# A hybrid RWKV-7 and convolution layer on one core: joined matmul bursts, the convolution moved forward, and dense products issued six at a time

## The chip, the cores and the metric

The kernel runs on one core of a Trainium2 chip. The metric is the time of one execution on the device in microseconds (us). Three timed runs of the kernel before took 1325.54, 1330.57 and 1337.1 us, and their median is 1330.57 us. TensorE, the matmul array, is called PE in the profile; VectorE is DVE, ScalarE is ACT, GpSimd is POOL, and SyncE (SP) issues the transfers.

## The reference

One layer for 640 tokens (512 latent and 128 context ones) of width 1024, cut to its products and the two branches:

```python
def _wkv(s0, r, w, k, v, a, b, reverse):
...
    def step(S, inp):
        rt, wt, kt, vt, at, bt = inp
        sa = jnp.einsum('bhvk,bhk->bhv', S, at)
        S = S * wt[:, :, None, :] + sa[..., None] * bt[:, :, None, :] + vt[..., None] * kt[:, :, None, :]
        return S, jnp.einsum('bhvk,bhk->bhv', S, rt)
...
    s_fin, ys = lax.scan(step, s0.astype(jnp.float32), xs, reverse=reverse)
...
def _conv_branch(glu_in, rows, lp):
    a, gt = jnp.split(glu_in, 2, axis=-1)
    u = a * jax.nn.sigmoid(gt)
...
    u = lax.conv_general_dilated(u, lp['conv_w'][:, None, :], (1,), [(CONV_K // 2, CONV_K // 2)],
                                 dimension_numbers=('NWC', 'WIO', 'NWC'), feature_group_count=C) + lp['conv_b']
...
    un = ((uf - mu) * lax.rsqrt(var + LN_EPS) * lp['conv_ln_g'] + lp['conv_ln_b']).astype(u.dtype)
    return jax.nn.silu(un) @ lp['w_out_conv']
...
    xn = _rmsnorm(x, lp['norm1_g']) * (1 + sc1) + sh1
    proj = xn @ lp['w_in']
    rkv, glu_in, gates = jnp.split(proj, [3 * RWKV_WIDTH, 3 * RWKV_WIDTH + 2 * CONV_WIDTH], axis=-1)
    gate_r, gate_c = jnp.split(gates, 2, axis=-1)
    y_r, s_f, s_b = _rwkv_branch(xn, rkv, s0_f, s0_b, lp)
    y_c = _conv_branch(glu_in, rows, lp)
    merged = jax.nn.sigmoid(gate_r) * y_r + jax.nn.sigmoid(gate_c) * y_c
    x = x + g1 * (merged @ lp['w_o'])
    xn2 = _rmsnorm(x, lp['norm2_g']) * (1 + sc2) + sh2
    h = jnp.square(jax.nn.relu(xn2 @ lp['mlp_w1']))
    x = x + g2 * (h @ lp['mlp_w2'])
```

## The kernel before

**Dense products.** Every product with a large weight is made in blocks of 128 output columns. Inputs and weights are split into a high and a low part, and each block is three products (high by high, low by high, high by low) over 8 slices of 128 inputs and two halves of 320 tokens, so a block is 48 matmuls of 128x128 by 128x320 (fewer inputs for the two branch outputs). In the profile they are the rows `ps_mm<-xh_t,wh_t` and the like. The rows `ps_mm<-ARGH_t,wh_t` are the products with the outputs of the two branches, called the sides: side "c" is the convolution's, side "r" the RWKV branch's.

**Lanes.** The scan is not run token by token: the 8 heads are taken as four pairs (p = 0 to 3), the tokens in chunks, and each pair goes through `prep` (operands), `gram` (products of operands), `inverse` (inverts 20 triangular matrices, in steps that go between DVE and PE), `builder` (five groups of chunks: matrices from `pb`, `pk`, `pl`, `pf`, `pu`), `chain` inside `scan` (the state is carried from chunk to chunk: `sp` makes a state, `po` an output) and `finish` (`post`: normalisation, bonus, gate). Their matmuls are small fp32 ones (32x32 to 128x128) in bursts of 4 to 40. The convolution (`conv_all`, five tiles of 128 tokens in `conv_tile`) and the modulation columns (`ada_late`) are lanes too. A lane is a generator that yields where it must wait for another engine.

**What sets the order.** All of this, from about 60 us until the sides' products, is recorded in one program order by a planner at build time: the loop at the end of the mixed stage picks a lane that can go on by its urgency, and otherwise takes one dense matmul from `filler` (through `more`), which works off the list `todo`. The order so found is fixed: on the chip each engine takes its instructions in that order and waits where an operand is not there. `todo` holds 36 blocks that need no lane beyond the projections' own (12 of r, k and v, 8 of the convolution's input `glu`, 16 gates), then the side blocks, which wait for the branches: `c` for its first two blocks, `r` for all the rest. Behind the mixed stage stands the MLP, dense blocks alone.

**Names.** `HEADS` and `QUADS` are halves and quarters of the 128 partitions; `GC` = 2 is the number of chunks in a group and direction; `rk[2, p]` is v of a pair; `hold()` and `let_go()` reserve the array's four result banks for one lane; `places` are buffers that weights may be split into. `GLU_AT` is the place in `todo` at which the four `glu` jobs stand.

```python
        while lanes:
            lane = pick(not hungry())
            if not lane and more():
                continue
            lane = lane or pick(True)
```

Of the kernel before, what the change touches and what calls it, by code (L numbers as in the profile page):

```python
# [10 lines left out]
F32 = mybir.dt.float32  # L11
# [47 lines left out]
RAWS, SPLITS, SWITCH, EXTRA = ["vr"], ["N1"], 1, 0  # L59
# [12 lines left out]
CST_ID, CST_MA, CST_MZ, CST_SEL, CST_HSEL, CST_LATE = 0, 128, 256, 512, 514, 516  # L72
NCST = 517
# [5 lines left out]
def hybrid_step(ctx: ExitStack, tc: tile.TileContext, I, O):  # L79
# [78 lines left out]
    mask_a = cst[:, CST_MA:CST_MA + 128]  # L158
# [458 lines left out]
    def ada_late(col):  # L617
# [10 lines left out]
        e = st([P, P], "ade")  # L628
        A.activation(e, ps, AF.Copy)
        yield  # L630
        ps = bank("t")[:, 0:2]
        mm(ps, e, sel)
        A.activation(mod[:, col, :], ps, AF.Identity, bias=pc("ada_b", col))
# [35 lines left out]
    def operands(p):  # L669
# [20 lines left out]
        for d in range(2):  # L690
# [46 lines left out]
            V.tensor_tensor(out=AB[:, ys, 3 * C:4 * C], in0=tv(at), in1=cs, op=ALU.mult)  # L737
# [16 lines left out]

    vr = wt([P, T], "vr")
# [14 lines left out]
    def gram(p):  # L770

        AB = grp[p]["AB"]
        N = grp[p]["N"] = wt([P, NY, C], f"N{p % 2}")
        yield from hold()
        for i, y0 in enumerate((0, 10)):
            ps = bank(BANKS[i])[:, 0:320].rearrange("p (y c) -> p y c", c=32)
            for y in range(y0, y0 + 10):
                for q, rows in enumerate(QUADS):
                    lo, h = HEADS[q // 2][0], 32 * (q % 2)
                    mm(ps[rows, y - y0, :], AB[lo, y, 2 * C + h:2 * C + h + 32], AB[lo, y, h:h + 32], tile_position=(lo.start, rows.start))  # L780
            A.activation(Gf[:, y0:y0 + 10, :], ps, AF.Copy)
            yield "A"
        for i, y0 in enumerate((0, 10)):
            ps = bank(UP_BANKS[i])[:, 0:320].rearrange("p (y c) -> p y c", c=32)
            for y in range(y0, y0 + 10):
                for s in range(2):
                    lo, rows = HEADS[s][0], QUADS[2 * s]
                    mm(ps[rows, y - y0, :], AB[lo, y, 2 * C:2 * C + 32], AB[lo, y, 32:64], tile_position=(lo.start, rows.start))
            for s in range(2):
                A.activation(N[QUADS[2 * s], y0:y0 + 10, 32:64], ps[QUADS[2 * s]], AF.Copy)  # L790
                yield "A"
        let_go()
        yield SEM
# [5 lines left out]
    def inverse(p):  # L799
# [68 lines left out]
        def products(lhsT, rhs, c0):  # L868
            ps = bank("t")[:, 0:160].rearrange("p (y j) -> p y j", j=16)
            for c in range(10):  # L870
                for q in QUADS:
                    mm(ps[q, c], lhsT[q, c0 + c, :], rhs[q, c0 + c, 0:16], tile_position=(q.start, q.start))
            return ps

        for c0 in (0, 10):
            A.activation(M[:, c0:c0 + 10], products(Gf, Nd, c0), AF.Copy, scale=late)
            yield
        for c0 in (0, 10):
            o = Nd[:, c0:c0 + 10, 0:16]
            V.tensor_tensor(out=o, in0=products(NT, M, c0), in1=o, op=ALU.add)  # L880
            yield

        def quads(f):

            ps = bank("t")[:, 0:320].rearrange("p (y c) -> p y c", c=32)
            for y in range(10):
                for s in range(2):
                    q0, q1 = QUADS[2 * s:2 * s + 2]
                    f(ps[q1, y, :], y, q0, q1)
            return ps  # L890

        for q in range(4):
            A.activation(N[QUADS[q], :, 32 * (q % 2):32 * (q % 2) + 32], Nd[QUADS[q], 0:NY, :], AF.Copy)
            yield "A"
        Tm = tmp.rearrange("p i x -> p (i x)")[:, 640:960].rearrange("p (y t) -> p y t", t=32)
        for y0 in (0, 10):
            ps = quads(lambda o, y, q0, q1: mm(o, Nd[q1, y0 + y, :], ident[q1, q1], tile_position=(q1.start, q1.start)))
            for s in range(2):
                q1 = QUADS[2 * s + 1]
                A.activation(NT[q1, y0:y0 + 10, :], ps[q1], AF.Copy)  # L900
            yield
            ps = quads(lambda o, y, q0, q1: mm(o, N[q0, y0 + y, 32:64], Nd[q0, y0 + y, :], tile_position=(q0.start, q1.start)))
            for s in range(2):
                q1 = QUADS[2 * s + 1]
                A.activation(Tm[q1], ps[q1], AF.Copy)
            yield
            ps = quads(lambda o, y, q0, q1: mm(o, NT[q1, y0 + y, :], Tm[q1, y, :], tile_position=(q1.start, q1.start)))
            for s in range(2):
                q0, q1 = QUADS[2 * s:2 * s + 2]
                A.activation(N[q1, y0:y0 + 10, 0:32], ps[q1], AF.Copy)  # L910
                G.memset(N[q0, y0:y0 + 10, 32:64], 0.0)
            yield
# [104 lines left out]
    def chain(p):  # L1017
# [6 lines left out]
        for g in range(5):  # L1024
# [3 lines left out]
            for i in range(GC):  # L1028
                if (g, i) == (3, GC - 1):
                    break  # L1030
# [620 lines left out]
```

## Time and profile before

| | us |
|---|---|
| median of three timed runs | 1330.57 |
| profiled execution | 1323.99 |
| its span | 1322.2 |
| PE busy in the span | 1236.1 (93%) |
| DVE busy | 654.0 (49%) |
| ACT busy | 505.3 (38%) |

The profiled execution is 6.6 us below the median. PE is busy for 93% of the span, and 86% of the chain that ended last lies on it, so the time is read as a sum along PE: what it does, at which clock, and where it stands still. The span has three parts: a prelude to about 60 us, the mixed stage to about 800 us, and the dense stage to 1320 us.

### The profile page before, as it was taken

To read this page: it belongs to the slowest core of one execution; us is meant where nothing else is said; L and a number is where in the kernel's file an instruction comes from. 1 tells how busy PE (TensorE), PEld (TensorE's weight loads), DVE (VectorE), ACT (ScalarE), POOL (GpSimd) and SP (SyncE) were. 2 spreads that over 40 slices of the span, in tenths; PEclk is the share of its full clock that TensorE was granted. 3 is DMA by queue.
4 is the path that set the end of the run, shared out by engine and by line. 5 is a ranking of instruction groups with operands and counts; after the bars stand their busy time and mean duration, and the time that the engine had idled before them with its cause. 6 is when DMAs were issued, how large, how long until landed. Compare 5 with 4: busy or idle time off the path is not lost.

```text
span 1322.2 us, 30685 instructions
## 1 busy us (share of the span) xinstructions
PE 1236.1 (93%) x13110; PEld 1094.7 (83%) x13110; DVE 654.0 (49%) x1342; ACT 505.3 (38%) x1149; POOL 31.4 (2%) x38
## 2 busy tenths in 40 slices
PE   8998899999999999999974899999999999999996
PEld 5776788777777878877741899999999999999996
DVE  5424575376465656245433566654443443443344
ACT  4445346436443643544212223344421331242130
POOL 0000000000000000100100000000000000000000
PEclk8989899999999999999976899989999999999998
DMA  9465433224222311231300683202222222222222
GB/s 371 144 207 171 149 117 122 78 67 150 80 78 81 124 43 58 87 92 54 100 26 8 209 286 122 74 32 78 73 75 81 72 72 81 80 71 74 81 73 80
DMA packets 77785, 136.14 MB, mean 103 GB/s; under 512 B 10768, under 2 KB 27824, under 8 KB 77648
## 3 DMA queue, kind: packets, MB, share of 16 engines
q1 hardware_dynamic: 77648, 134.17, 30.9%
q8 instruction: 103, 1.69, 0.5%
q14 instruction: 34, 0.28, 0.1%
HBM read 112.90 MB, written 21.23 MB: 101 GB/s over the span
## 4 chain that ended last, share of the span: by engine, by line
PE 86%; DVE 4%; ACT 3%; issue 3%; DMA 2%; SPq 0%; POOL 0%; POOLq 0%; DVEq 0%; ACTq 0%
PE ps_mm L195 45%; PE ps_b L195 21%; PE ps_t L195 12%; PE ps_a L195 6%; PE ps_ad L195 2%; DMA z<-tmp 1%; ACT Nb_w L108 1%; DMA par_t<-in_par 1%; DVE E_w L108 1%; DVE Gt_w L108 1%; ACT tmp L108 0%; DVE ARGH_t L108 0%; DMA g<-tmp 0%; DVE Gf_w L108 0%; ACT N_w L108 0%
## 5 line engine op out<-in xcount | busy, mean ns | idle before, releaser
L195 PE MATMUL ps_mm<-xh_t,wh_t 128*128 128x320 f32 x664 | 219.9, 331 | 1.2 <-ACT tmp L108 1.2
L195 PE MATMUL ps_mm<-xl_t,wh_t 128*128 128x320 f32 x664 | 219.8, 331 | 0.0
L195 PE MATMUL ps_mm<-xh_t,wl_t 128*128 128x320 f32 x664 | 217.1, 327 | 0.0
L108 ACT ACTIVATE wh_t<-wr_t 128x512 fp32r<-128x512 f32 x150 | 94.3, 629 | 141.0 <-PE ps_b L195 107.7
L108 DVE TENSOR_TENSOR wl_t<-wr_t,wh_t 128x512 fp32r<-128x512 f32 x150 | 102.8, 686 | 90.6 <-ACT wh_t L108 90.4
L195 PEld LDWEIGHTS ps_mm<-xh_t,wh_t 128*128 128x128 f32 x664 | 128.1, 193 | 19.8 <-issue 14.4
L195 PEld LDWEIGHTS ps_mm<-xl_t,wh_t 128*128 128x128 f32 x664 | 128.2, 193 | 14.6 <-issue 10.8
L195 PEld LDWEIGHTS ps_mm<-xh_t,wl_t 128*128 128x128 f32 x664 | 127.9, 193 | 12.4 <-issue 9.0
L195 PE MATMUL ps_mm<-ARGH_t,wh_t 128*128 128x320 f32 x284 | 77.8, 319 | 11.7 <-ACT wh_t L108 10.9
L108 ACT ACTIVATE tmp<-ps_mm 128x320 f32<-128x320 f32 x80 | 34.9, 436 | 96.7 <-PE ps_mm L195 90.8
L195 PE MATMUL ps_mm<-ARGH_t,wl_t 128*128 128x320 f32 x212 | 67.4, 318 | 0.0
L195 PEld LDWEIGHTS ps_mm<-ARGH_t,wh_t 128*128 128x128 f32 x284 | 53.1, 199 | 12.4 <-ACT wh_t L108 11.1
L108 ACT ACTIVATE mwh<-wr_t 128x512 fp32r<-128x512 f32 x49 | 31.1, 634 | 74.5 <-PE ps_b L195 69.9
L108 DVE TENSOR_TENSOR mwl<-wr_t,mwh 128x512 fp32r<-128x512 f32 x49 | 33.8, 690 | 38.6 <-ACT mwh L108 38.6
L108 DVE TENSOR_TENSOR tmp<-tmp 128x320 f32<-128x320 f32 x64 | 31.2, 489 | 42.7 <-ACT tmp L108 42.7
L108 DVE SCALAR_TENSOR_TENSOR ARGH_t<-ps_mm,mod_t,ARGH_t 128x320 f32<-128x320 f32 (+2 forms) x45 | 22.6, 511 | 59.4 <-PE ps_mm L195 59.4
L195 PE MATMUL ps_mm<-xl,wh_t 128*128 128x320 f32 x140 | 43.9, 314 | 0.0
L195 PE MATMUL ps_b<-ARGH_t,wl_t 128*128 128x320 f32 x140 | 43.2, 308 | 0.0
L195 PE MATMUL ps_b<-xl,wh_t 128*128 128x320 f32 x140 | 43.1, 308 | 0.0
L195 PE MATMUL ps_b<-ARGH_t,wh_t 128*128 128x320 f32 x140 | 42.6, 304 | 0.0
L195 PEld LDWEIGHTS ps_mm<-ARGH_t,wl_t 128*128 128x128 f32 x212 | 41.5, 196 | 0.4 <-DVE wl_t L108 0.4
L108 DVE SCALAR_TENSOR_TENSOR ARGH_t<-ps_b,mod_t,ARGH_t 128x128 f32<-128x128 f32 (+1 forms) x75 | 26.3, 390 | 20.0 <-PE ps_b L195 20.0
(372 smaller groups left out, 3027.6 us busy)
## 6 DMA issues: line engine op xcount, KB each, us to landing
wr_t<-in_w SPq DMA_DIRECT2D x225, 256.0 KB, 2.8
adl_w<-in_adal SPq DMA_DIRECT2D x64, 256.0 KB, 3.3
adar_s<-in_adaw SPq DMA_DIRECT2D x16, 512.0 KB, 8.4
ARGH_t<-in_x SPq DMA_DIRECT2D x8, 640.0 KB, 5.8
z<-tmp SPq DMA_DIRECT2D x32, 160.0 KB, 3.0
gate<-tmp SPq DMA_DIRECT2D x32, 160.0 KB, 1.8
tA_t<-z SPq DMA_DIRECT2D x8, 320.0 KB, 3.4
ath_t<-z SPq DMA_DIRECT2D x8, 320.0 KB, 3.4
```

What stands on the lines that cost most here:

```text
L108: return f(*args, **kw)
L195: PE.matmul(out=out, lhsT=lhsT, rhs=rhs, start=start, stop=stop, **kw)
```

## The change

- `todo`: the four `glu` jobs stand at place 3 and not 12, right behind the first pair's projections.
- The main loop: where it takes a dense matmul, it takes up to six in a row (`STAY`).
- The convolution runs as soon as `glu` is done: `conv_tile` works in the tiles `pa`, `pg`, `N1` and `cy` and writes its result to memory (`conv0` to `conv3`); a new lane `conv_branch` loads it again later, splits it and opens side "c". `solve(p)`, which runs `gram` and `inverse`, waits for a first mark of the convolution (its constants), and for pair 1 also until all five tiles are done; `finish` waits for the tiles too.
- Bursts are joined: `gram` issues its 120 matmuls in one burst of four rows where it had four bursts; `inverse` joins each pair of products (80 matmuls instead of 2 of 40), makes its transposes with one DVE operation per pair instead of 8 bursts of PE, and has two bursts of 40 where it had four of 20 beside those; `build` issues v, `pb`, `pk` and `pl` in one burst (v reversed is not made any more: the operand is stored reversed, and two masks depend on the direction); `chain` issues a chunk's state and output products together; `ada_late` adds four columns at a time.

```diff
+STAY = 6
...
-GLU_AT = 12
+GLU_AT = 3
...
-        for i, y0 in enumerate((0, 10)):
-            ps = bank(BANKS[i])[:, 0:320].rearrange("p (y c) -> p y c", c=32)
-            for y in range(y0, y0 + 10):
-                for q, rows in enumerate(QUADS):
-                    lo, h = HEADS[q // 2][0], 32 * (q % 2)
-                    mm(ps[rows, y - y0, :], AB[lo, y, 2 * C + h:2 * C + h + 32], AB[lo, y, h:h + 32], tile_position=(lo.start, rows.start))
-            A.activation(Gf[:, y0:y0 + 10, :], ps, AF.Copy)
-            yield "A"
+        for y in range(NY):
+            for q, rows in enumerate(QUADS):
+                lo, h = HEADS[q // 2][0], 32 * (q % 2)
+                mm(near[y // 10][rows, y % 10, :], AB[lo, y, 2 * C + h:2 * C + h + 32], AB[lo, y, h:h + 32], tile_position=(lo.start, rows.start))
+        for y in range(NY):
+            for s in range(2):
+                lo, rows = HEADS[s][0], QUADS[2 * s]
+                mm(far[y // 10][rows, y % 10, :], AB[lo, y, 2 * C:2 * C + 32], AB[lo, y, 32:64], tile_position=(lo.start, rows.start))
...
+        V.transpose(out=NT, in_=Nd)
...
+        for q, ys, ps in quads(BANKS, lambda o, y, q0, q1: mm(o, N[q0, y, 32:64], Nd[q0, y, :], tile_position=(q0.start, q1.start))):
+            A.activation(Tm[q, ys], ps, AF.Copy)
...
-            ps = quads(lambda o, y, q0, q1: mm(o, Nd[q1, y0 + y, :], ident[q1, q1], tile_position=(q1.start, q1.start)))
...
     def solve(p):
-        while p not in operated or (p and p - 1 not in inverted) or (p > 1 and p - 2 not in built):
+        while p not in operated or len(convolved) < 1 + (p == 1) or (p and p - 1 not in inverted) \
+                or (p > 1 and p - 2 not in built):
             yield 0.3
...
     def finish(p):
-        while p and p - 1 not in scanned:
+        while len(convolved) < 2 or (p and p - 1 not in scanned):
...
-        while 3 not in inverted:
-            yield 0.5
...
-        while 2 not in built or 3 not in operated:
-            yield 0.3
...
+        convolved.append(0)
+        for i in range(4):
+            while i not in gated_linear:
+                yield 1.0
...
+            yield from conv_tile(i, u, ut, pr)
+        convolved.append(1)
+        spawn(conv_branch(), URGENT["branch"])
...
+    def conv_branch():
+
+        while 2 not in built or 3 not in operated:
+            yield 0.3
+        un = st([P, 2, 4, T], "ARGH", 2, F32R)
+        for j in range(4):
+            t = st([P, T], f"ath{j % 2}")
+            DMA.dma_start(out=t, in_=dram(f"conv{j}"))
+            yield 2.5 if j == 0 else 0.5
+            split(un[:, 0, j, :], un[:, 1, j, :], t)
...
             if not lane and more():
+                for _ in range(STAY - 1):
+                    if not more():
+                        break
                 continue
```

In all PE has 9251 matmuls and not 9411 (the 160 transposes are gone), and its order changes between dense and lane matmuls 320 times and not 617 times; the dense matmuls are the same 5712. SP issues 24 transfers more (20 writes of the convolution's tiles and 4 loads).

On PE, at the first pair's `gram` (`ps_a<-ARGH_t 32x32` and `ps_b<-ARGH_t 32x32`; the other rows are dense products), before:

```order
L195 MATMUL ps_mm<-xh_t,wh_t 128x320
L195 MATMUL ps_a_1468<-ARGH_t 32x32 x40
L195 MATMUL ps_mm<-xl_t,wh_t 128x320
L195 MATMUL ps_b_1512<-ARGH_t 32x32 x40
L195 MATMUL ps_mm<-xh_t,wl_t 128x320
L195 MATMUL ps_a_1555<-ARGH_t 32x32 x20
```

and now:

```order
L197 MATMUL ps_mm<-xh_t,wl_t 128x320
L197 MATMUL ps_a_1383<-ARGH_t 32x32 x40
L197 MATMUL ps_b_1384<-ARGH_t 32x32 x40
L197 MATMUL ps_a_1385<-ARGH_t 32x32 x20
L197 MATMUL ps_b_1386<-ARGH_t 32x32 x20
L197 MATMUL ps_mm<-xh_t,wh_t 128x320
```

The four bursts stand together, without a dense product between them. For pairs 0, 1, 2 and 3 the burst stood behind 409, 717, 996 and 1263 dense matmuls (counting the first 144 of small projections); now it stands behind 414, 1326, 1554 and 1872, and 1872 are all that need neither side.

On PE, where the 36 blocks end, before: the last row of a gate block stands just ahead of these, with the first of two convolution tiles; here are the second tile (`cf_w` are the convolution's matrices) and the first product of side "c":

```order
L195 MATMUL ps_t<-cst_t,Nb_w 128x128 x4
L195 MATMUL ps_t<-cst_t,prod_w 128x128 x4
L195 MATMUL ps_t<-Nb_w,cf_w 128x512 x2
L195 MATMUL ps_t<-Gf_w,cf_w 128x512
L195 MATMUL ps_t<-Gt_w,cf_w 128x512
L195 MATMUL ps_t<-Gf_w,cf_w 128x512
L195 MATMUL ps_t<-Gt_w,cf_w 128x512
L195 MATMUL ps_t<-cst_t,Nb_w 128x128 x4
L195 MATMUL ps_mm<-ARGH_t,wh_t 128x320 x2
```

and now, from the last gate product on, with pair 2's `inverse` (two joined products, two joined quads) and the start of the first group of its `build` (v, then `pb` and `pk`):

```order
L197 MATMUL ps_mm<-xh_t,wl_t 128x320
L197 MATMUL ps_t<-Gt_w,Gf_w 32x16 x80
L197 MATMUL ps_t<-Gf_w,prod_w 32x16 x80
L197 MATMUL ps_a_6729<-Gt_w,N_w 32x32 x20
L197 MATMUL ps_b_6730<-Gt_w,N_w 32x32 x20
L197 MATMUL ps_a_6787<-Gf_w,prod_w 32x32 x20
L197 MATMUL ps_b_6788<-Gf_w,prod_w 32x32 x20
L197 MATMUL ps_b_6846<-cst_t,vS_w 64x64 x8
L197 MATMUL ps_a_6855<-M_w,ARGH_t 64x128
L197 MATMUL ps_b_6856<-M_w,ARGH_t 64x128
```

Behind the 36 blocks there stood 28 matmuls of convolution ahead of side "c"; now there stand 939 lane matmuls (the end of pair 2's `inverse`, its five groups of `build` with their `chain`, pair 3's `gram`, pair 2's `post`, and the start of pair 3's `inverse`), then the 96 of side "c" in three pieces, and then 335 lane matmuls more (pair 3's `build`, `chain` and `post`).

On PE, where those 939 matmuls end, now: pair 2's `post`, pair 3's `inverse`, and the first product of side "c":

```order
L197 MATMUL ps_ad<-S_w,M_w 64x64 x4
L197 MATMUL ps_ad<-M_w,S_w 64x64 x4
L197 MATMUL ps_t<-Y_w,cst_t 64x320 x4
L197 MATMUL ps_t<-cst_t,pa_t 128x2 x5
L197 MATMUL ps_t<-cst_t,rh_t 64x128 x10
L197 MATMUL ps_t<-Gt_w,Gf_w 32x16 x80
L197 MATMUL ps_t<-Gf_w,prod_w 32x16 x80
L197 MATMUL ps_a_7819<-Gt_w,N_w 32x32 x20
L197 MATMUL ps_b_7820<-Gt_w,N_w 32x32 x20
L197 MATMUL ps_mm<-ARGH_t,wh_t 128x320 x2
```

Side "c" moved ahead of pair 3's `build`; side "r" still comes last of all.

## Rows read from the trace of the kernel before

**Rows 1.** The page: its span, and PE's granted clock in 40 slices, in tenths.

```profile
span 1322.2 us, 30685 instructions
PEclk8989899999999999999976899989999999999998
```

**Rows 2.** Stretches: length, busy us (instructions) of each engine, PE clock, DMA share, GB/s.

```profile
627.00:673.00 46.00, 44.53 (x302) 35.03 (x300) 18.60 (x35) 11.73 (x25) 3.96 (x3) 1.00 0.27 88
673.00:730.00 57.00, 25.59 (x66) 11.81 (x64) 20.34 (x38) 13.36 (x26) 1.09 (x2) 0.60 0.05 15
730.00:747.00 17.00, 16.96 (x97) 16.58 (x96) 6.41 (x13) 2.81 (x5) 0.00 (x0) 0.83 0.63 184
747.00:800.00 53.00, 49.17 (x325) 47.51 (x325) 34.85 (x70) 15.21 (x30) 0.00 (x0) 1.00 0.76 254
800.00:1322.00 522.00, 509.43 (x3469) 508.41 (x3467) 240.52 (x488) 165.92 (x325) 3.41 (x4) 0.98 0.24 76
```

**Rows 3.** The same view, one stretch inside the dense stage.

```profile
880.00:920.00 40.00, 40.00 (x277) 40.00 (x276) 20.10 (x38) 17.71 (x39) 0.00 (x0) 1.00 0.23 73
```

**Rows 4.** The timeline of PE, a lane's bursts among dense products: start, length, idle before.

```profile
588.25 0.31 PE L195 MATMUL ps_mm<-xh_t,wl_t 128*128 128x320 f32 x1
...
588.49 0.69 PE L195 MATMUL ps_ad<-M_w,S_w 128*64 128x64 f32 x16
...
589.11 0.32 PE L195 MATMUL ps_a<-M_w,ARGH_t 64*64 64x128 f32 x1
...
590.14 0.41 PE L195 MATMUL ps_mm<-xh_t,wh_t 128*128 128x320 f32 x1
...
590.92 0.34 PE L195 MATMUL ps_t<-cst_t,ARGH_t 64*64 64x64 f32 x4
...
592.04 0.41 PE L195 MATMUL ps_mm<-xl_t,wh_t 128*128 128x320 f32 x1
```

**Rows 5.** The timeline of PE, ACT and DVE, the rest of that group.

```profile
592.53 1.09 PE L195 MATMUL ps_a<-ZB_w,N_w 64*64 64x128 f32 x16
...
593.73 0.60 ACT L108 ACTIVATE RB_w<-ps_a 128x512 f32<-128x512 f32 x1 [1.91 <-PE ps_a L195]
...
597.42 0.37 PE L195 MATMUL ps_a<-RB_w,L_w 64*128 64x128 f32 x1
...
598.31 0.27 PE L195 MATMUL ps_b<-RB_w,L_w 64*128 64x128 f32 x1
...
598.62 0.69 DVE L108 TENSOR_TENSOR M_w<-ps_a,M_w 128x512 f32<-128x512 f32 x1 [5.74 <-PE ps_b L195]
...
600.61 0.45 PE L195 MATMUL ps_ad<-S_w,M_w 128*64 128x64 f32 x8
601.00 0.41 PE L195 MATMUL ps_mm<-xh_t,wh_t 128*128 128x320 f32 x1
```

**Rows 6.** Two timeline rows of DVE: the first and last stream transposes of pair 0's inverse.

```profile
156.85 2.02 DVE L108 STREAM_TRANSPOSE Gt_w<-Gf_w 128x1024 f32<-128x1024 f32 x1
...
177.76 2.05 DVE L108 STREAM_TRANSPOSE prod_w<-Nb_w 128x1024 f32<-128x1024 f32 x1
```

**Rows 7.** Lines by form, 405 to 630 us, pairs 2 and 3: the transposes on PE.

```profile
L195 PE MATMUL ps_t<-cst_t,Gt_w 32*32 32x32 f32 x160 | 3.3, 192 | 0.4 <-DVE Y_w L108 0.4
```

**Rows 8.** The timeline of PE at pair 2's gram, and a stretch just behind it.

```profile
359.60 0.51 PE L195 MATMUL ps_a<-ARGH_t 64*32 64x32 f32 x20 [1.65 <-issue]
```

```profile
360.40:363.80 3.40, 3.40 (x50) 3.01 (x48) 0.00 (x0) 2.20 (x6) 0.00 (x0) 0.51 0.03 5
```

**Rows 9.** Timeline of PE: one burst of eight transposes, ahead of 673 us and behind.

```profile
672.12 1.05 PE L195 MATMUL ps_t<-cst_t,Nb_w 128*128 128x128 f32 x8
...
693.12 2.04 PE L195 MATMUL ps_t<-cst_t,Nb_w 128*128 128x128 f32 x8 [3.19 <-DVE Nb_w L108]
```

**Rows 10.** Two stretches around 673 to 747 us, columns as in Rows 2.

```profile
710.00:720.00 10.00, 5.20 (x16) 2.45 (x14) 2.08 (x6) 1.51 (x3) 0.54 (x1) 0.84 0.00 1
730.00:740.00 10.00, 9.96 (x50) 9.76 (x50) 3.90 (x8) 2.81 (x5) 0.00 (x0) 0.71 0.49 149
```

More of the change, by code (lines that the diff above doesn't have):

```diff
@@ L866, in inverse, with products @@
         M = Gf.rearrange("p u t -> p (u t)")[:, 0:320].rearrange("p (y j) -> p y j", j=16)
-        def products(lhsT, rhs, c0):
-            ps = bank("t")[:, 0:160].rearrange("p (y j) -> p y j", j=16)
-            for c in range(10):
+        def products(lhsT, rhs):
+            ps = bank("t")[:, 0:320].rearrange("p (y j) -> p y j", j=16)
+            for y in range(NY):
                 for q in QUADS:
-                    mm(ps[q, c], lhsT[q, c0 + c, :], rhs[q, c0 + c, 0:16], tile_position=(q.start, q.start))
+                    mm(ps[q, y], lhsT[q, y, :], rhs[q, y, 0:16], tile_position=(q.start, q.start))
@@ L873, in products @@
             return ps
[L875 to L886, printed above, removed]
-                for s in range(2):
-                    q0, q1 = QUADS[2 * s:2 * s + 2]
-                    f(ps[q1, y, :], y, q0, q1)
-            return ps
+        A.activation(M, products(Gf, Nd), AF.Copy, scale=late)
@@ new lines, in inverse, with quads @@
+        yield
+        o = Nd[:, 0:NY, 0:16]
+        V.tensor_tensor(out=o, in0=products(NT, M), in1=o, op=ALU.add)
+        yield "V"
+        V.transpose(out=NT, in_=Nd)
+        Tm = Gf.rearrange("p u t -> p (u t)")[:, 0:NY * 32].rearrange("p (y t) -> p y t", t=32)
+        def quads(banks, f):
+            ps = [bank(b)[:, 0:320].rearrange("p (y c) -> p y c", c=32) for b in banks]
+            for y in range(NY):
+                for s in range(2):
+                    f(ps[y // 10][QUADS[2 * s + 1], y % 10, :], y, *QUADS[2 * s:2 * s + 2])
+            return [(q, slice(10 * i, 10 * i + 10), ps[i][q]) for i in range(2) for q in QUADS[1::2]]
@@ L896, in inverse @@
-        for y0 in (0, 10):
-            ps = quads(lambda o, y, q0, q1: mm(o, Nd[q1, y0 + y, :], ident[q1, q1], tile_position=(q1.start, q1.start)))
[L898 to L912, printed above, removed]
+        for q, ys, ps in quads(UP_BANKS, lambda o, y, q0, q1: mm(o, NT[q1, y, :], Tm[q1, y, :], tile_position=(q1.start, q1.start))):
+            A.activation(N[q, ys, 0:32], ps, AF.Copy)
+            yield "A"
@@ L938, in build @@
                     V.memset(S[lo, s, :, 0, :], 0.0)
-            t = last[0] + SEM
+            yield max(0.0, last[0] + SEM - now[0])
             yield from hold()
@@ L979, in build @@
             A.activation(RB, pf, AF.Copy)
-            yield max(t, last[0] + SEM) - now[0]
+            yield
             pu = [bank(b) for b in BANKS]
@@ L1104, in conv_all @@
         DMA.dma_start(out=cf, in_=I["cf"])
-        for i in range(4):
-            while i not in gated_linear:
-                yield 1.0
-        while 3 not in inverted:
-            yield 0.5
         ew = wt([P, 2 * P + W], "prod")[0:32]
@@ L1265, in ada_all @@
     def ada_all():
+        e = wt([P, 4, P], "ade")
         for c in range(16, 48):
-            yield from ada_late(c)
+            yield from ada_late(c, e)
     def fill():
```

191 lines of the change are left out of this document (93 added, 98 removed).

## The prediction

> **What bounds the kernel now.** I read the page first. PE is busy for 93% of the span of 1322.2 us, and its clock row is at or near full but for a hollow at slices 21 and 22 [rows 1]. So the time is a sum along PE, and the question for each part of the change is where PE stands still and at which clock it works. The stretches show the hollow [rows 2]: up to 673 us PE is busy nearly all the time (44.53 of the last 46 us). From 673 to 730 us it is busy for 25.59 of 57 us at a mean clock of 0.60, with 66 instructions. The 36 blocks that need no side are used up there, and two convolution tiles stand alone in PE's order. At 730 us side "c" starts (17 us for its 96 matmuls), then side "r" and the MLP up to the end. I call these three parts E (up to the end of the 36 blocks, 673 us now), S (from there to side "r", 74 us) and R (from 747 us on, 575 us). Inside R a stretch of 40 us shows 277 dense matmuls at full clock, 0.1444 us each [rows 3].
>
> In the mixed stage I read the timeline for two prices. The first is that of a switch: between dense matmuls one starts every 0.144 us, but the lane's burst starts 0.24 us behind the last dense one, and the first dense one behind a burst takes 0.41 us where its fellows take 0.31 [rows 4]. That is 0.10 + 0.10, so I take 0.185 us (estimate) for a visit to a lane. The second price is the bursts themselves, start to next start: 0.62 us (16 records of `po`), 1.03 us (`pb`, `pk`), 1.12 us (`pl`) [rows 4]; 1.09 us (`pf`), 0.89 + 0.27 = 1.16 us (`pu`), 0.39 us (one `sp`) [rows 5]; v is 0.6 us, half of `pl`, which has twice its products. A group of `build` with its two steps of `chain` is 0.6 + 1.03 + 1.12 + 1.09 + 1.16 + 2 x 0.39 + 0.62 = 6.4 us of PE.
>
> **The change part by part: what E loses.** (1) The order changes 320 times between dense and lane and not 617 times, so 148 visits go: 148 x 0.185 = 27 us. Nearly all of them lie ahead of 673 us, on PE. (2) The transposes on PE go: 3.3 us for pairs 2 and 3 [rows 7], so 6.6 us for four. Each pair pays a DVE transpose of 2.05 us for it [rows 6], in a lane beside dense work, which hides it; without that cover it is 2 us. (3) Bursts that are joined lose a gap each. The one of 1.65 us inside `gram` [rows 8] is the largest: its last four rows are one burst now, and a stretch at clock 0.51 stands behind that gap. I take 8 us for all of these, between 0 and 15. (4) The operand stored reversed, the second mask, the DVE adds of four columns at a time and the fewer ACT copies: 0, as DVE (49%) and ACT (38%) are not what PE waits for in E; in S a DVE operation would show, and the counts change there by less than one in a hundred. The 20 writes and 4 loads of the convolution on SP's queue come when transfers take 5 to 76% of the DMA engines [rows 2]: 0, at most 5 us if a weight's load stands behind them. (5) The two convolution tiles that stood behind 673 us move ahead of it: 9 us of PE at full clock.
>
> (6) The largest term is in the order. At pair 2's `gram` PE has made 1554 of the 1872 dense matmuls that need no side, and had made 996; at pair 3's, all 1872, against 1263. The reasons are in the code: six dense products at a time, bursts of a lane less often, and pair 1's `gram` behind all five convolution tiles (1326 dense matmuls ahead of it, 717 before). So the dense work runs out early, and behind its last product stand 939 lane matmuls, where 28 stood. What now lies behind the 36 blocks is ten groups of `build` and `chain` (64 us at 6.4), two joined inversions' ends and one `gram` (about 13 us, each burst of 40 to 80 at the 0.8 us per ten rounds of [rows 7]), and two `post`: 80 us of PE. These leave E. E = 673 - 27 - 6.6 - 8 + 9 - 80 = 560 us.
>
> **What S becomes.** S is now a chain of lanes with no dense product to fill their waits. A group at full clock is its 6.4 us of PE and what it waits for: ACT's `RB` (0.60 us) between `pf` and `pu`, two DVE adds (0.69 us each) behind `pu`, both in [rows 5], two copies of the state in `chain` and the latencies of these hand-overs, together 3.2 us: 9.6 us. At half clock PE's part doubles, as a burst of eight transposes shows, 1.05 us before 673 us and 2.04 us behind it [rows 9]: 12.8 + 3.2 = 16 us. Ten groups are 96 or 160 us. The rest of S: the end of pair 2's `inverse` (8 us), pair 3's `gram` and the DVE part of its `inverse` (from the first stream transpose to the last 23 us for pair 0 [rows 6], among other work; with pair 2's `post` between them, and the first group overlapping, I take 30), the end of that `inverse` (8), side "c" (96 x 0.144 = 14), the last `chain` and `post` (11), loads and splits of side "r" (5): 76 us at full clock, some 89 at half, since the DVE part does not change. S is 172 us at full clock and 249 at half.
>
> Which clock? A lane chain of this kind is what stood in the hollow: short bursts, then a wait for DVE or ACT. PE ran there at a mean of 0.60, that is, a fifth of the time at full clock and the rest at half. One long burst lifted it for a moment (0.84 in the stretch from 710 us), and dense work brought it back within the ten microseconds from 730 us (0.71) [rows 10]. Even in the mixed stage a gap of 1.65 us among bursts stood just ahead of a stretch at 0.51 [rows 8]. The new S is made of the same kind of pieces as the hollow, a burst of 1 to 3 us and then a hand-over to DVE or ACT and back, so I take the hollow's mixture: with a fifth of the time at full clock, S is 1 / (0.8/249 + 0.2/172) = 228 us.
>
> The rule that speaks against this is in the Trainium skill, TensorE: Matmul & The Clock Gate, "HAM oscillation": the clock falls back when a long wait separates the bursts. By that rule the waits of a group, all short, would leave the clock up, and the sum would be rival 1's; the same page's "A second HAM failure mode" has short idles between groups of matmuls drop it too, and [rows 8] agrees with that one.
>
> **The sum.** R stays 575 us, and the clock that falls at the end of S costs its start some 4 us (as at 730 us): 579. The span is 560 + 228 + 579 = 1367 us, against 1322.2: 45 us longer. The profiled execution is 1323.99 us with 1.8 us around the span, which gives 1369; the median stands 6.6 us above that execution, inside the three runs' spread, so that 1369 to 1375 is meant. I say 1370 us.
>
> **Rivals.** Rival 1, the clock stays up in S: S is 172, R 576, the span 1308, the time 1310 us, faster. For it: joined bursts are longer (2.75 us for v, `pb`, `pk` and `pl` together), and a long one lifted the clock. Against it: the hollow, the one place in this trace where lanes stood without dense products, was at half for four fifths of its time.
>
> Rival 2, the clock is at full for half of S: 203 us in S, 1344 us. It is what long bursts would give if each lifted the clock until the next.
>
> Rival 3, the waits shown as work hidden elsewhere are shorter, and the lanes run nearly at PE's rate, so that the hollow is closed and only the savings remain: 1324 - 57 - 27 - 15 + 9 = 1234 us, much faster. It needs dense products beside pair 2's and 3's `build`, and the order has none there; I see no way to it but an S that overlaps its two lanes (pair 3's `inverse` beside pair 2's `build`), which could take 30 us at most.
>
> Rival 4, on the slow side of the forecast: half clock throughout S, 249 us, and E at 570 because the joined waits cut less: 1400 us.
>
> **How the numbers follow.** The forecast and rival 4 together hold 0.70 (0.58 and 0.12), rival 2 0.13, rival 1 0.13, rival 3 0.04. A measurement of this kernel tells about 1% from no change, 13 us. Faster by more (under 1317 us): rivals 1 and 3, less the part of rival 1 that a slower E would bring back to within 1%, 0.15. Within 1% (1317 to 1344): half of rival 2, and that part, 0.12. Slower: the rest, 0.73. The unknown terms are E (560, 545 to 572) and S's clock (172 to 249 us). The range leaves out rivals 1 and 3 and the far end of rival 4: 1320 to 1400 us.
>
> **What would show it.** In the changed kernel's profile the 36 blocks should end at 545 to 572 us; behind them a stretch of about 170 us should show PE busy for well under 90% with a clock of 0.5 to 0.7, the rows of `ps_a<-M_w,ARGH_t` 14 to 16 us apart from group to group; then the 96 matmuls of side "c", and a second such stretch. Side "r" should start near 790 us, with 579 us to the end. The waits ahead of `ps_ad` and `ps_a` rows should be for ACT and DVE, with no dense rows beside them. The prediction is wrong if the clock row stays at 9 through that stretch (rival 1), or if the 36 blocks end much later than 572 us, which would mean that the lanes were slower in the mixed stage and that the dense products lasted longer than the order's counts say.

## The result, and the profile after

The changed kernel takes 1399.81 us (median of four runs, 1397.24 to 1402.09) where the kernel before takes 1328.17 us; the ratio is 1.0526, with an interval of 1.0471 to 1.0582. It is slower, by 72 us. The forecast was 1370 us in a range of 1320 to 1400 us; the median lies inside it by 0.2 us.

The page of the changed kernel, with the rows that answer to [rows 1] and its row of PE:

```profile
span 1399.7 us, 30058 instructions
PE 1240.4 (89%) x12790; PEld 1116.5 (80%) x12790; DVE 662.0 (47%) x1354; ACT 491.1 (35%) x1096; POOL 29.7 (2%) x30
PE   8987999898988899977658659999999999999997
PEclk9999989898999999977759869999999999999998
```

PE is busy for about as long as before (1236.1 us then) in a span that is 77 us longer. The hollow of [rows 1] is wider and begins earlier: slices 18 to 24 of the clock row, with one slice near full among them.

The same three stretches of both kernels, E, S and R of the prediction, as in [rows 2] (length, busy us of PE, PEld, DVE, ACT and POOL, PE clock, DMA). Before:

```profile
60.00:673.70 613.70, 580.47 (x8803) 471.83 (x8802) 319.16 (x659) 279.16 (x697) 25.53 (x27) 0.97 0.32 103
673.70:747.00 73.30, 41.85 (x157) 27.68 (x155) 26.75 (x50) 15.74 (x30) 1.09 (x2) 0.65 0.18 54
747.00:1322.20 575.20, 558.60 (x3791) 555.91 (x3790) 275.37 (x557) 181.13 (x354) 3.41 (x4) 0.99 0.28 92
```

And after:

```profile
60.00:610.60 550.60, 487.90 (x5829) 404.67 (x5828) 252.05 (x520) 204.40 (x477) 18.50 (x15) 0.94 0.33 107
610.60:824.20 213.60, 135.99 (x2807) 115.52 (x2806) 101.55 (x202) 74.73 (x194) 6.40 (x6) 0.73 0.19 58
824.20:1399.70 575.50, 561.05 (x3792) 558.22 (x3792) 275.70 (x557) 181.57 (x355) 3.40 (x4) 0.98 0.27 90
```

The last gate product starts at 610.6 us (E, 673.7 before), side "r" at 824.2 us (747 before), and the rest takes 575 us in both. Of the 77 us, E gave 63 back and S took 140.

For the comparison below I split the time from 60 us to side "r" of each kernel into three. **Work** is what PE's records would take at full clock (their busy time, less half of what lies under a clock record of 0.5); **idle** is time without a record on PE; **clock** is that half, the time that half clock cost. The rows above give the same roughly: a stretch of length L at mean clock c spent 2 x (1 - c) x L at half. Work, idle and clock are those of the one execution that was profiled; the last column is the median of all executions of a run.

| kernel | 60 us to side r | work | idle | clock | median us |
|---|---|---|---|---|---|
| before | 687.0 | 592.5 | 64.7 | 29.8 | 1328.2 |
| changed | 764.2 | 558.8 | 140.3 | 65.1 | 1399.8 |
| e1 STAY = 1 | 746.9 | 560.7 | 123.2 | 63.0 | 1384.6 |
| e2 joined bursts alone | 730.0 | 559.5 | 106.9 | 63.7 | 1360.0 |
| e3 joined bursts and STAY = 6 | 770.0 | 555.2 | 143.1 | 71.7 | 1404.9 |
| e4 spare products | 765.1 | 612.3 | 103.8 | 49.0 | 1402.2 |
| e5 as e2, copies behind | 676.5 | 557.8 | 78.4 | 40.3 | 1308.2 |
| e6 as e5, gram and inverse apart | 671.0 | 571.9 | 70.8 | 28.3 | 1308.4 |
| e7 before, joined chain alone | 712.0 | 596.5 | 83.2 | 32.3 | 1351.9 |
| e8 changed, copies behind | 723.1 | 557.4 | 112.1 | 53.6 | 1355.3 |
| e9 as e5, convolution early elsewhere | 668.4 | 560.7 | 72.7 | 35.0 | 1304.2 |
| e10 as e8, STAY = 1 | 679.2 | 564.7 | 81.2 | 33.3 | 1315.8 |
| e11 as e9, STAY = 6 | 728.0 | 554.1 | 113.5 | 60.3 | 1365.6 |
| e12 as e9, gram and inverse apart | 638.2 | 581.0 | 49.1 | 8.1 | 1291.7 |

The runs were taken in five sessions, in which the median of the kernel before lay between 1322.9 and 1328.5 us, so a difference of a few us between two runs tells nothing. In e12 two of the four executions were over 1.5% slower than the fastest, and the profile is of the fastest, so that its median stands 16 us above its row of the account.

So the change does what it says: 33.7 us less work for PE. It pays with 75.6 us of idle time and 35.3 us of half clock.

Who PE waited for in the changed kernel, 60 to 824 us (total us, times, longest):

```profile
PE ps_ad L197 <- ACT S_w L109: 22.0, 32, 1.0
PE ps_t L197 <- issue: 12.6, 7, 2.5
PE ps_ad L197 <- DVE M_w L109: 11.5, 20, 2.3
PE ps_t L197 <- DVE cy_w L109: 9.6, 4, 2.9
```

The first row is new: the kernel before has no wait of `ps_ad` for `S_w` in its rows of PE's waits from 60 to 747 us. The timeline of PE and ACT in a lane-only stretch shows what it is:

```profile
639.93 0.56 ACT L109 ACTIVATE S_w<-ps_ad 64x128 f32<-64x128 f32 x2 [1.58 <-PE ps_ad L197]
...
640.54 0.69 PE L197 MATMUL ps_ad<-M_w,S_w 128*64 128x64 f32 x8 [0.65 <-ACT S_w L109]
...
641.02 0.64 PE L197 MATMUL ps_ad<-S_w,M_w 128*64 128x64 f32 x8
641.71 0.56 ACT L109 ACTIVATE S_w<-ps_ad 64x128 f32<-64x128 f32 x2 [0.69 <-PE ps_ad L197]
642.31 0.69 PE L197 MATMUL ps_ad<-M_w,S_w 128*64 128x64 f32 x8 [0.66 <-ACT S_w L109]
```

`ps_ad<-S_w,M_w` is the state product, `S_w<-ps_ad` the ACT copy of the new state, `ps_ad<-M_w,S_w` the output product of the same chunk. The output product needs the old state only, yet it starts 0.04 to 0.05 us behind the end of the copies, and PE stands still for them, 0.65 us here and 0.69 us in the mean. In the code the copies now stand between the two; in the kernel before, the state products of a group's two chunks came first and the output products behind them. In the trace all 32 waits stand ahead of an output product, one for each step of the four pairs that copies a state (8 a pair). That holds for the second chunk of a group too, whose copies write another state tile than the one that its output product reads. What state product, copy and output product share in both chunks is the result tile `ps_ad`.

### The profile page after: what moved, and what is told of

It is laid out like the page before. It is cut to its first block, busy times and chain, and to the rows that moved or that the text cites. A ratio compares the mean times of both kernels' runs of the same rounds, so it can differ in the third digit from the quotient of the medians.

```text
span 1399.7 us, 30058 instructions
## 1 busy us (share of the span) xinstructions
PE 1240.4 (89%) x12790; PEld 1116.5 (80%) x12790; DVE 662.0 (47%) x1354; ACT 491.1 (35%) x1096; POOL 29.7 (2%) x30
## 4 chain that ended last, share of the span: by engine, by line
PE 59%; DVE 4%; issue 3%; ACT 3%; DMA 1%; POOL 0%; POOLq 0%; DVEq 0%; ACTq 0%; SPq 0%
PE ps_mm L197 29%; PE ps_b L197 20%; PE ps_t L197 5%; PE ps_a L197 3%; PE ps_ad L197 2%; ACT S_w L109 1%; DVE M_w L109 1%; DVE Y_w L109 1%; ACT N_w L109 0%; DVE Gt_w L109 0%; DMA u_t<-gate 0%; DVE ARGH_t L109 0%; POOL rh_t L109 0%; DMA ARGH_t<-in_x 0%; ACT RB_w L109 0%
## 5 line engine op out<-in xcount | busy, mean ns | idle before, releaser
L197 PE MATMUL ps_mm<-xh_t,wh_t 128*128 128x320 f32 x680 | 232.0, 341 | 4.0 <-ACT tmp L109 4.0
L197 PE MATMUL ps_mm<-xl_t,wh_t 128*128 128x320 f32 x680 | 215.6, 317 | 0.0
L197 PEld LDWEIGHTS ps_mm<-xh_t,wh_t 128*128 128x128 f32 x680 | 132.8, 195 | 42.0 <-issue 32.0
L109 DVE TENSOR_TENSOR wl_t<-wr_t,wh_t 128x512 fp32r<-128x512 f32 x154 | 105.7, 687 | 117.3 <-ACT wh_t L109 116.9
L197 PEld LDWEIGHTS ps_mm<-xh_t,wl_t 128*128 128x128 f32 x680 | 132.8, 195 | 2.0 <-DVE wl_t L109 2.0
L197 PEld LDWEIGHTS ps_mm<-xl_t,wh_t 128*128 128x128 f32 x680 | 133.3, 196 | 0.9 <-issue 0.5
L197 PE MATMUL ps_mm<-ARGH_t,wh_t 128*128 128x320 f32 x300 | 83.3, 326 | 12.7 <-ACT wh_t L109 11.9
L197 PE MATMUL ps_mm<-ARGH_t,wl_t 128*128 128x320 f32 x220 | 70.4, 320 | 0.0
L197 PEld LDWEIGHTS ps_mm<-ARGH_t,wh_t 128*128 128x128 f32 x300 | 56.7, 202 | 13.8 <-ACT wh_t L109 12.3
L197 PE MATMUL ps_ad<-M_w,S_w 128*64 128x64 f32 x320 | 20.5, 259 | 23.5 <-ACT S_w L109 22.0
```

The lines of the kernel that those rows point to most:

```text
L109: return f(*args, **kw)
L197: PE.matmul(out=out, lhsT=lhsT, rhs=rhs, start=start, stop=stop, **kw)
```

## The experiments

Two theories went in. A: the order spends the dense products early, and lanes without them are slow. B: the joined bursts, or the convolution in front of pair 1's `gram`, cost by themselves. They need not exclude each other; the runs were to say how much each holds.

**e1, six in a row undone.**

```diff
-STAY = 6
+STAY = 1
```

> The changed kernel with STAY = 1, all else kept: one dense product at a time, as before. Its order leaves 255 + 319 lane matmuls without dense products (939 + 335 in the changed kernel). Theory A (the order: dense products spent early leave the lanes alone): the stretch from the last gate block to side r falls from 214 us to about 14 + 200 x 574/1274 = 104 us, and the 36 blocks end later, at about 610 + 44 = 655 us, since that lane work moves ahead of them; time 655 + 104 + 575 + 2 = 1336 us (1315 to 1350). Rival B (the joined bursts and the convolution in front of pair 1's gram cost by themselves, whatever the number of dense products in a row): at least 1375 us.

1384.56 us (ratio to before 1.0441, 1.0371 to 1.0510). Only 15 us came back. As A had said, E ended later (665.7 us) and S was shorter (141 us, not 104), but 59 us to the kernel before stayed open: A's range (1315 to 1350) failed and B's number (1375 or more) came.

**e2, the joined bursts alone.**

```diff
-GLU_AT = 3
+GLU_AT = 12
-        while p not in operated or len(convolved) < 1 + (p == 1) or (p and p - 1 not in inverted) \
+        while p not in operated or (p and p - 1 not in inverted) \
-        while len(convolved) < 2 or (p and p - 1 not in scanned):
+        while p and p - 1 not in scanned:
```

with `conv_all` and `conv_tile` as before and STAY = 1.

> The changed kernel with STAY = 1 and the convolution put back where it was (GLU_AT = 12, no wait for it in solve and finish): of the change only the joined bursts are left. No lane-only stretch in its order, 203 switches from lane to dense instead of 308. Theory A: faster than before: 105 x 0.185 = 19 us for switches, 6.6 us for the transposes and up to 8 us for gaps, with the hollow of 57 us kept: about 1324 - 33 = 1291 us (1280 to 1305). Rival B: no gain or a loss, 1320 us or more, because long bursts of small matmuls stand still inside (the gap inside gram grew from 1.65 to 3.24 us).

1360.05 us (1.0251, 1.0189 to 1.0312). Theory A's number fell, and B's side held: this part of the change alone makes the kernel slower. Its work fell by 33 us (the expectation had 19 + 6.6 us of work and 8 of gaps), while idle time rose by 42 and the clock's share by 34. B's reason, stands inside long bursts, is the smaller part: in the four bursts of `gram` they are 10.5 us, and 6.6 us in the kernel before. The first row of PE's waits names the larger (e2, 60 to 780 us):

```profile
PE ps_ad L197 <- ACT S_w L109: 23.1, 32, 2.8
```

**e3, the convolution late, six in a row kept.** e2 with STAY = 6.

> The changed kernel with the convolution put back where it was (GLU_AT = 12, no wait for it in solve and finish) and STAY = 6 kept. Its order has 914 lane matmuls without dense products behind the gate blocks. Theory A (six in a row is what spends the dense products early): slow still, 590 us to the last gate block, 190 us of lanes, some 40 us of convolution and side c, 575 behind: about 1395 us (1365 to 1420). Rival D (the convolution put in front of pair 1's gram is what spends them): at or under 1345 us.

1404.94 us (1.0579, 1.0507 to 1.0651). As A said: no dense product from 581 to 814 us. Six in a row spends the dense products early wherever the convolution stands; against e2 it costs 45 us.

**e4, spare products in the lane-only stretches.**

```diff
+                if len(todo) <= 8 and not jobs and len(chained) < 4:
+                    if not spare:
+                        spare.append(bank())
+                    while now[0] < goal:
+                        mm(spare[0][:, 0:P], ident, ident)
```

> The changed kernel with 204 spare products (identity by identity, 128x128 fp32, into a bank that nobody reads; no result of the computation changes) put at the points of the lane-only stretches where PE would wait by the order's planner. They add about 204 x 0.26 = 53 us of PE work at full clock, in time in which PE stood still (98 us of it between 611 and 824 us). If the clock sets the length of these stretches, it stays near full and the 214 us fall to about 185: 1370 us (1358 to 1385). If the hand-overs between PE, DVE and ACT set it, the stretch stays at 214 us or grows by up to 40 us: 1398 to 1440 us.

1402.24 us (1.0570, 1.0511 to 1.0629), the same as the changed kernel. S of e4:

```profile
615.60:825.10 209.50, 168.11 (x3214) 146.41 (x3213) 101.88 (x202) 74.17 (x194) 6.61 (x6) 0.89 0.20 59
```

The clock was 0.89 there and not 0.73, the stretch took 209.5 us against 213.6, and the kernel's time did not change, as the expectation had it for hand-overs that set the length. It does not follow that the hand-overs alone set the length of S. Here are three groups of `build` of pair 2 (first row) and three of pair 3 (second row), in the changed kernel and then in e4:

```profile
630.50:666.70 36.20, 26.90 (x430) 23.63 (x429) 22.20 (x38) 18.16 (x54) 0.00 (x0) 0.74 0.07 20
757.60:788.10 30.50, 20.63 (x438) 17.39 (x436) 13.56 (x28) 13.20 (x43) 0.00 (x0) 0.96 0.01 2
```

```profile
634.20:664.50 30.30, 26.32 (x466) 22.26 (x464) 21.80 (x36) 17.26 (x51) 0.00 (x0) 1.00 0.06 15
752.60:789.40 36.80, 32.11 (x540) 28.34 (x538) 13.56 (x28) 13.20 (x43) 0.00 (x0) 1.00 0.03 9
```

For pair 2 the clock rose from 0.74 to 1.00, and three groups took 5.9 us less. For pair 3 the clock was near full in both kernels, and with the spare products three groups took 6.3 us more. Ahead of a state product there the changed kernel stands still for 0.71 us, and e4 has a run of spare products that lasts 2.05 us:

```profile
775.14 0.33 PE L197 MATMUL ps_ad<-S_w,M_w 128*64 128x64 f32 x2 [0.71 <-DVE M_w L109]
```

```profile
772.52 2.05 PE L197 MATMUL ps_mm<-cst_t 128*128 128x128 f32 x16
```

Over all of S the clock's share fell from 36.4 to 12.8 us, and spare products and idle time together took 19.5 us more than the idle time alone had. So the clock did matter in S, and the spare products took back what it gave. What S would take at full clock without them no run shows. The 98 us of the expectation is what the column of weight loads (PEld) leaves of S; PE itself stood still for 77.6 us.

**e5, e2 with the copies of the state behind the output products.**

```diff
+                for d in range(2):
+                    t0 = C * (GC - 1 - i if d else i)
+                    for s in range(2):
+                        mm(po[64 * s:64 * s + 64, d, t0:t0 + C], S[:, s, d, i, :], M[:, s, d, i, 64:128])
                 if step and (g, i) != (4, GC - 1):
...
-                for d in range(2):
-                    t0 = C * (GC - 1 - i if d else i)
-                    for s in range(2):
-                        mm(po[64 * s:64 * s + 64, d, t0:t0 + C], S[:, s, d, i, :], M[:, s, d, i, 64:128])
```

> As the run with the joined bursts alone (1360 us), but in the chain the two ACT copies of the state stand behind the output products and not between the state products and them, so the output products have no wait for ACT any more. Theory E (that wait, 0.65 us of PE standing still in each of 31 to 36 steps, and the clock that falls with it, is most of what the joined bursts lost): 24 us of idle time and some 15 us of half clock go, 1321 us (1305 to 1335), no slower than the kernel before. Rival F (the joined bursts of gram and inverse, which now hold all four result banks, delay the lanes and so the convolution behind them): 1345 us or more.

1308.17 us (0.9886, 0.9807 to 0.9965): 52 us less for four lines that change places, more than theory E had asked. PE's waits of e5, 60 to 780 us, begin with

```profile
PE ps_t L197 <- DVE E_w L109: 11.3, 3, 3.9
PE ps_mm L197 <- ACT wh_t L109: 11.1, 1, 11.1
PE ps_b L197 <- issue: 9.7, 5, 3.4
```

and the row of `S_w` is gone. Idle time fell by 28.5 us (the 32 waits were 23.1) and the clock's share by 23.4: with the stands inside the lanes went half clock. The planner made a somewhat different order too (pair 3's `gram` stands behind 1444 dense products and behind 1476 in e2), so e7 below tests the wait in the other direction.

**e6, gram and inverse apart again in e5.** `gram` and the second half of `inverse` as in the kernel before.

> As the one above, and the bursts of gram and inverse are apart again as in the kernel before (four bursts in gram; products, transposes and quads in inverse on PE, in one bank); build, chain and the modulation columns stay joined. Theory E: within 15 us of the one above (their work on PE is some 8 us more, their waits less). Rival F: at least 25 us faster than the one above, at or below 1300 us, with pair 3's gram near 460 us again (535 us with the joined bursts alone).

1308.39 us (0.9893, 0.9818 to 0.9968). The same time as e5, so theory E holds and F's number falls. The account shows two things that cancel: 14 us more work, 8 less idle and 12 less for the clock. Pair 3's `gram` came at 450 us (500 in e5, 535 in e2), and, as I read it, the hollow behind the gate blocks, still there in both, hid that (e12 below tests it).

**e7, the kernel before with the joined chain alone.**

```diff
-                if (g, i) == (3, GC - 1):
-                    break
+                step = (g, i) != (3, GC - 1)
...
+                for d in range(2):
+                    t0 = C * (GC - 1 - i if d else i)
+                    for s in range(2):
+                        mm(po[64 * s:64 * s + 64, d, t0:t0 + C], S[:, s, d, i, :], M[:, s, d, i, 64:128])
```

> The kernel before with one part of the change: the chain's state and output products joined per chunk, as in the changed kernel, with the copies between them. Theory E: some 36 waits of 0.65 us of PE for ACT, 24 us, and a few us of half clock: 1350 us (1340 to 1368). Rival F: no loss, 1318 to 1333 us.

1351.88 us (1.0209, 1.0137 to 1.0280), inside theory E's range. This one part of the change, put into the kernel before, costs 29 us, in nearly the same order (pair 3's `gram` behind 1260 dense products, and 1263 before); the wait is there with the same numbers:

```profile
PE ps_ad L195 <- ACT S_w L108: 22.9, 32, 1.3
```

**e8, the changed kernel with the copies behind.** The diff of e5.

> The changed kernel with the two ACT copies behind the output products. Theory E: 22 us of PE waits for these copies go (10.5 us ahead of the end of the gate blocks, 11.5 us behind it), and some half clock: 1373 us (1358 to 1384). Rival F: 1390 us or more.

1355.30 us (1.0237, 1.0167 to 1.0307), 44.5 us less than the changed kernel and 3 us below theory E's range: the copies held more than it asked.

**e9, the convolution early in tiles of its own.** e5's chain, STAY = 1, and

```diff
-        while p not in operated or len(convolved) < 1 + (p == 1) or (p and p - 1 not in inverted) \
+        while p not in operated or len(convolved) < 1 or (p and p - 1 not in inverted) \
...
-        while len(convolved) < 2 or (p and p - 1 not in scanned):
+        while p and p - 1 not in scanned:
...
-        u, ut = [st([P, W], tag) for tag in ("pa", "pg")]
-        pr = wt([P, 2, W], "N1")
+        while 3 not in prepared:
+            yield 0.3
+        u, ut, *pr = [st([P, T], tag)[:, 0:W] for tag in ("ath0", "ath1", "tB", "pt0")]
```

with GLU_AT = 12 and the convolution's urgency at 0.7.

> The joined bursts with the ACT copies behind the output products (1308 us), STAY = 1, and the convolution early in another way: it starts when pair 3's operands are made, in tiles that only the making of operands used (ath0, ath1, tB, pt0), so that neither pair 1's gram nor post waits for it. Its order has no lane-only stretch, pair 3's gram stands behind 1353 dense products (1872 in the changed kernel), and behind the last gate product side c follows at once. Theory A (what was left of the loss, 1355 against 1308 us, is the order: dense products spent while the lanes wait for the convolution): the hollow of 67 us closes and some 10 us of convolution move ahead of it: 1252 us (1240 to 1270). Rival H (a convolution run early costs its waits wherever it stands): 1295 us or more.

1304.25 us (0.9844, 0.9801 to 0.9887): faster than before by 1 to 2%. The 4 us to e5 are not clear of noise (the two intervals overlap). Theory A's 1252 us missed, and the time is on rival H's side (1295 us or more). The gate blocks ended 29 us later than in e5, and then PE waited once for 21.6 us:

```profile
PE ps_mm L197 <- ACT wh_t L109: 23.7, 2, 21.6
```

In the timeline of e9 the last convolution tile and pair 3's `post` end at 692 and 698 us, behind the last dense product (681.6 us): the lanes came in too late, and a stretch S of 47 us, from 681.6 us on, took the place of one of 84 in e5. That the late lanes and not the convolution's own waits are the reason is argued here; e12 tests it.

**e10, e8 with STAY = 1.**

> The changed kernel with the ACT copies behind the output products (1355 us) and STAY = 1; the convolution still in front of pair 1's gram. Lane-only stretches of 210 and 335 matmuls (859 and 335 with STAY = 6). Theory A1 (the convolution in front of pair 1's gram holds the larger part of the 47 us that are left): 1340 us (1325 to 1350). Rival A2 (six in a row holds it): 1318 us or less.

1315.85 us (0.9926, 0.9888 to 0.9963): 39.5 us less than e8, so A2 and not A1. Six in a row holds nearly all that the copies had left; for the convolution in front of pair 1's `gram` the 8 us to e5 remain, which are not clear of noise (the intervals overlap).

**e11, e9 with STAY = 6.**

> As the first of these three, with STAY = 6: a single difference. Its order has a lane-only stretch of 698 matmuls behind the gate blocks. Theory A: that stretch takes some 110 us in which no dense product runs, and the gate blocks end about 50 us earlier: 1310 us (1285 to 1330), 40 us or more over the first. Rival G (six in a row saves switches and costs nothing): within 12 us of the first.

1365.60 us (1.0310, 1.0262 to 1.0359): 61 us over e9, so G fell and A's "40 us or more" came; the time lies above A's range (1330 at most). The gate blocks ended 89 us earlier than in e9, not 50. Its rows, to set beside those of e12:

```profile
60.00:592.30 532.30, 492.86 (x7144) 427.96 (x7144) 265.91 (x530) 224.39 (x543) 16.70 (x12) 0.94 0.35 111
592.30:788.00 195.70, 121.56 (x1474) 80.70 (x1473) 88.20 (x189) 57.00 (x133) 8.18 (x9) 0.75 0.18 54
```

**e12, e9 with gram and inverse apart.**

> The convolution early in tiles of its own and STAY = 1, as in the run of 1304 us, with the bursts of gram and inverse apart as in the kernel before (as in the other run of 1308 us); build, chain and the modulation columns joined, copies behind the output products. In its order pair 3's post stands behind 1585 and the last convolution tile behind 1754 of the 1872 dense products; with the joined inverse they stood behind 1872 and 1849, that is, at the end, and side c waited 31 us for them. Theory I (joined inverse: its quads hold all four result banks and so push the lanes back by some 290 dense products; without a hollow behind them nothing hides that): the wait ahead of side c goes, side c follows the gate blocks at 662 us, 1255 us (1243 to 1272). Rival J (the convolution costs as much idle and half-clock time among the dense products as it did behind them): 1290 us or more.

1291.7 us (0.9747, 0.9692 to 0.9802); its executions took 1275.8 to 1298.6 us. The profiled one is the fastest, so that its rows show the best of it:

```profile
60.00:660.30 600.30, 566.37 (x8753) 462.56 (x8752) 334.26 (x692) 279.29 (x672) 22.65 (x28) 0.99 0.34 108
660.30:698.20 37.90, 22.72 (x202) 19.96 (x200) 16.16 (x29) 9.04 (x20) 1.97 (x1) 0.89 0.55 170
```

It is the fastest kernel of the study: its slowest execution is below the fastest of e9 (1302.4 us). In the profiled executions it has 20 us more work than e9 and 24 us less idle and 27 us less half clock: the first stretch runs at 0.99. Theory I had the direction, and its number (1255) was 37 us too low. By the median the time is on rival J's side (1290 us or more), by two of four executions it is not, so the time does not decide; against J speaks that idle time and half clock fell as they did with the convolution still among the dense products. A wait of 11.8 us for the first weights of side "c" stayed, and why the clock differs from run to run (0.963 to 0.981) is open.

## Why the prediction was right, and where it was not

The forecast was slower by 45 us, the result slower by 72 to 77 us, at the upper end of the range. The direction and its main reason came: dense products spent early, and lanes alone behind them. The size is inside the range by luck: the median by 0.2 us, with two of the four executions above 1400, and E was 51 us longer than forecast while S was 14 us shorter and R 4. By the prediction's own sign, "if the 36 blocks end much later than 572 us", this step of it was wrong. Its terms against the trace:

- **E: 560 us forecast, 610.6 measured.** The work came out as summed: 33.7 us less up to side "r", against 27 + 6.6. What failed is what E waits for: idle time in E rose from 33.2 to 62.7 us and the clock's share from 16.7 to 28.7. Term 3 had "Bursts that are joined lose a gap each ... I take 8 us". One join, that of the chain, added a wait instead (22.0 us in 32 waits, 10.5 us of it ahead of 610.6 us). The gaps inside `gram` did not go either: without a releaser in the trace PE stood still for 1.89, 1.60, 1.65 and 1.45 us in the four pairs before (so that the 1.65 us of [rows 8] are not the largest), and for 2.09, 3.23, 1.28 and 0 us now, 6.6 us in both. The timeline of PE at pair 1's `gram` in the changed kernel:

```profile
442.70 0.57 PE L197 MATMUL ps_a<-ARGH_t 64*32 64x32 f32 x26
446.51 0.38 PE L197 MATMUL ps_a<-ARGH_t 64*32 64x32 f32 x13 [3.23 <-issue]
```

  Term 4 took ACT and DVE as 0, "not what PE waits for in E". PE's idle time in E that ended with one of them was 23.5 us before and is 50.2 us now. Half clock was not in the sum for E at all: PE was busy at half for 57.3 us there against 33.3 before, for less work. The early convolution added 9.6 us, waits of other lanes for bank `ps_t` while a tile's DVE steps held it (`cy_w` in the rows of waits).
- **S: 228 us forecast, 213.6 measured.** The stretch is there, with side "c" in it as the order said. The terms behind the number came close. PE's work is 99.6 us (80 and side "c" 14 forecast) and its idle time 77.6, together 177.2 us, against 172 at full clock. The clock cost 36.4 us where the forecast had 56, since it was 0.73 and not 0.60, and not evenly so. Groups of `build` were 11.5 to 13.0 us apart at the start of it (630.5, 643.4, 655.1, 666.7 us) at 0.74, between my 9.6 and 16; pair 3's were 15.7 (with a piece of side "c"), 9.9, 10.0 and 10.6 us apart, the last three at 0.96. That the clock sets the length between the two agrees with pair 2's groups in e4 (9.6 to 10.4 us at 1.00). Rival 1's condition, a clock that stays up, was not met, and no run without spare products shows what it would have given.
- **R: 579 forecast, 575.5 measured.**
- **What the order term carries.** From the changed kernel to e5 the runs lead in three steps: copies behind, 1399.8 to 1355.3; STAY = 1, to 1315.8; the convolution late, to 1308.2. That is 44.5 + 39.5 + 7.7 us of 91.6. By another path the shares are others: STAY = 1 first (e1) gives 15.2 us, and the copies then 68.8 (e1 to e10). The two losses are not independent, and no single share can be given: the wait cost 29 to 69 us in its four comparisons and six in a row 15 to 61 us in its four. The prediction put the whole loss on the order. The order is a large part (e11 against e9: 61 us without the wait), and the wait in the chain is another of its size. That wait I did not see, although the code shows the copies between the two products.
- **The chances.** They do not add up as the prediction splits them: half of rival 2 and the 0.02 taken from rival 1 give 0.085 within 1%, not 0.12, and leave 0.765 for slower, not 0.73.
- **Rivals 2 to 4.** None came: the time is at rival 4's, 1400, but by the waits in E and not by half clock throughout S. The rule on long waits (the Trainium skill, TensorE: Matmul & The Clock Gate, "HAM oscillation") would have left the clock up among the short waits of a group; it was at half for 117 of the 213.6 us of S, but the clock was 0.96 in pair 3's groups, which have waits of the same kind and stand behind the dense products of side "c". The same page's "A second HAM failure mode", frequent short idles between groups of matmuls that make the clock fall and rise, agrees with e2 against e5, where the clock cost 63.7 and 40.3 us.

What is open: why the burst of `gram` stands still, why the clock stayed up in pair 3's groups and not in pair 2's, what S would take at full clock, and the spread of e12.

## What to carry to other kernels

When products on one engine are moved together, look at what stands between them on the other engines: a copy out of a result bank that was harmless behind the group becomes a wait inside it, and the fix here was four lines in another order. A saving in busy time is not a saving in time: set up the account of work, idle and clock for both kernels, and ask each term separately. Filler work that is independent is a stock that must last as long as the chains that it covers; issuing it in larger portions ended it 36 to 93 us earlier here and cost 15 to 61 us.

## What the runs showed of the hardware

32 stands of about 0.7 us inside lanes, 22 to 27 us in all, went with more than their own length of time: 29 us when put into the kernel before (e7), 44.5, 52 and 69 us when taken out (e8, e2 to e5, e1 to e10). Part of the rest is clock: its cost fell by 23 us from e2 to e5.

A burst of small matmuls stood still in its middle, with no releaser in the trace: 3.2 us in the `gram` shown above, behind 187 of its 240 records. It does so joined and apart, but less apart: over the four pairs 9.1 us in e5 and 7.0 in e6 (one stand of 2.1 us there is ahead of a dense product between the bursts), 9.3 in e9 and 2.5 in e12.

Spare products raised the granted clock from 0.73 to 0.89 over 210 us and changed the time of the kernel by less than 0.2%. Where the clock had been 0.74 the lanes became faster with them, and where it had been 0.96 slower.
